# Layer 0's first FFN output projection: both halves token-major, the last half turned behind a joint gate pair

## The chip, the cores and the metric

The kernel runs on one core of a Trainium2 chip. The metric is the device time of one execution in microseconds (us); the time before is the median of 3 runs. TensorE (PE) multiplies, its weight load (PEld) overlaps the product before; VectorE (DVE), ScalarE (ACT) and GpSimd (POOL) do the elementwise work; SyncE (SP) issues nearly all DMAs. Weights come from DRAM, products are summed in PSUM banks of 512 fp32 columns.

## The reference

A two-layer decoder trunk on 256 tokens of width 1024. Cut to what matters here, layer 0 is

```python
h = h + 0.5 * swiglu_ffn(rmsnorm(h, ffn1_norm[0]), ffn1_w_in[0], ffn1_w_out[0])   # (silu(gate) * up) @ w_out
hn = rmsnorm(h, mix_norm[0])
b_gate, c_gate, v = jnp.split(hn @ conv_w_in, 3, axis=-1)
u = c_gate * v
y = causal_conv3(u, conv_w)            # width 3, one filter per channel
h = h + (b_gate * y) @ conv_w_out
h = h + 0.5 * swiglu_ffn(rmsnorm(h, ffn2_norm[0]), ffn2_w_in[0], ffn2_w_out[0])
```

Layer 1 has a shared K/V projection, two FFNs of the same kind and sparse attention in place of the convolution. d_ff is 2816, which is 22 blocks of 128.

## The kernel before

**Number format.** Every fp32 product is made of three: each operand is split into a high part rounded to fp32r and the rest, and high x high, rest x high and high x rest are summed. A weight "unit" is 128 x 1024 fp32 weights as such a pair (wh, wl).

**Weights.** The class `Stream` (object `W`) loads chunks of two units (1 MB) from DRAM into three buffers `ws` by SP (L139), rounds a unit on ScalarE (`high`, CAST, L166) and takes the rest on VectorE (`low`, L183). Six units are held at most. `W.take()` hands one to the products, `W.done(n, pump)` gives buffers free and, unless told not to, calls `W.pump()`, which rounds units until the buffers are full; a chunk's load is issued when the last unit of the chunk two before it is rounded. All engines run their instructions in the order in which the program writes them (a manual schedule), so a place in the code is a place in each engine's queue.

**Two forms of product.** Channel-major: a weight tile of 128 x 128 stands in the array and all 256 tokens of both parts of the activations pass (512 columns, L539), then the weight's rest with the high parts (256 columns, L545). Token-major: 128 tokens stand in the array and 512 weight columns pass, three times (L485 to L487 in `out_proj`). A token-major result has tokens on partitions and must be turned: VectorE transposes blocks of 32 x 32 (L493), two DMAs write the tile to DRAM (`back`, L494), two read it back with channels on partitions (`come`, L513), and `joined(m)` adds channel tiles 2m and 2m+1 to the residual `h` (L520).

**Layer 0's first output projection.** `out_proj` with `rest` and without `whole`: `half` makes the first 512 channels token-major; tiles 4 to 7 of the other 512 are channel-major, each evacuated from PSUM by `out_evac` (L455), with `come` and `joined(0)`, `joined(1)` put between them. Layer 1's first projection (which comes after layer 0's second FFN) already runs with `whole=True`: both halves token-major, `joined(2)` and `joined(3)` called later, between joint products of the K/V projection, where each channel gets two sets of norm inputs (`xkv` and `xs`).

**The norm.** `Norm.high` and `Norm.low` write the scaled activations `xs[c]` in two parts (L294 on ScalarE, L298 on VectorE); `squares` squares on ScalarE (L309) and sums on GpSimd (L311); `halves` splits the sum (L317, L318 on GpSimd); `rows` sums over channels on TensorE (L327) and takes the root and the reciprocal R (L329, L331).

**The convolution's products.** Four token-major groups (c_gate and v, `conv_tokens`, 8 channel tiles k each, one unit per two k), each in a pair of PSUM banks `mm` of which there are two pairs, then eight channel-major tiles for b_gate. `conv_step(n, k)` puts the side work into these loops: the norm's rows in group 0 and the DMA round trip that makes the column form r2 of R (L774, L775), `conv_turned` (evacuates, scales with r2, transposes, L747 to L752), `placed` (reads back), `conv_taps` (the filter).

Of the kernel before, what the change touches and what calls it, by code (L numbers as in the profile page):

```python
# [16 lines left out]
P = 128  # L17
T = 256
# [50 lines left out]
def trunk(ctx, tc, A, out):  # L69
# [30 lines left out]
    def bank2():  # L100
        return mk([P, 2, 512], "mm", 2, pool=ps)
# [366 lines left out]
        if c == ND - 1:  # L468
            norm.low(c)

    def out_proj(lhs, factor, norm, rest=None, cut=(7, 7, 7, 2), whole=False):

        n, i, u = len(lhs), 0, None

# [35 lines left out]
        def come(new=t2):  # L510
            for m in range(2):
                came.append(new([P, 2, T], F32))
                sy.dma_start(came[m].rearrange("p c (b j) -> p c b j", j=32),  # L513
                             d[m].rearrange("t (b i) (x c j) -> (i x) c (t b) j", i=32, c=2, j=32))

        def joined(m):
            cs = range(2 * m, 2 * m + 2)
            u = came.pop(0)
            for c in cs:
                ve.scalar_tensor_tensor(out=h[c], in0=u[:, c % 2], scalar=factor, in1=h[c], op0=ALU.mult, op1=ALU.add)  # L520
            for c in cs:
                norm.high(c)
            for c in cs:
                norm.squares(c)
                norm.low(c)
# [22 lines left out]

        if whole:
            d = half(lambda k: come() if k == 6 else joined(k // 3 - 4) if k in (12, 15) else None)  # L550
            W.pump()
            come(act)
            return joined

        c = 4
# [163 lines left out]
    hid, rest = ffn_tokens(xs, rc=rc, n0=2, hid=hid, old=old)  # L719
    xs = new_xs()  # L720
    nm = Norm([(xs, G_MIX)])
    out_proj(hid, 0.5, nm, rest=rest)
    nm.halves()

    zs, Y, conv = [], [], {}
    tab = tables()
# [1 line left out]
    def conv_tokens(o, step):  # L728

        for k in range(8):  # L730
            if k % 2 == 0:
                u, = W.take()
            wh, wl = [u[x][:, (k % 2) * 512:(k % 2 + 1) * 512] for x in range(2)]
            for tt in range(2):
                sh, sl = xs[k][:, tt * P:(tt + 1) * P], xs[k][:, T + tt * P:T + (tt + 1) * P]
                pe.matmul(o[:, tt], sh, wh, start=(k == 0), stop=False)  # L736
                pe.matmul(o[:, tt], sl, wh, start=False, stop=False)
                pe.matmul(o[:, tt], sh, wl, start=False, stop=(k == 7))  # L738
            if k % 2 == 1:
                W.done(1, k < 7)  # L740
            step(k)

    def conv_turned(o):
        tb = t2([P, 2, T])
        for tt in range(2):
            g = t1()
            ac.copy(g, o[:, tt, :T])  # L747
            ve.scalar_tensor_tensor(out=g, in0=o[:, tt, T:], scalar=conv["r2"][:, tt:tt + 1], in1=g,
                                    op0=ALU.mult, op1=ALU.mult)
# [18 lines left out]
        po.tensor_tensor(out=y, in0=y, in1=conv["R"], op=ALU.mult)  # L768

    def conv_step(n, k):  # L770
        if (n, k) == (0, 5):
            conv["R"] = R = nm.rows()
            rd, rc, conv["r2"] = mk([1, T], "rd", 1, pool=dr), mk([P, 2], "rc", 2, pool=tiny), sm([P, 2])
            sy.dma_start(rd, R[:1])  # L774
            sy.dma_start(rc, rd.rearrange("o (t p) -> (o p) t", t=2))  # L775
            po.tensor_tensor(out=conv["r2"], in0=rc, in1=rc, op=ALU.mult)
        if (n, k) in ((1, 1), (2, 2)):
            next(tab)
        if (n, k) == (1, 4):
            way.append(conv_turned(conv.pop("o")))  # L780
        if (n, k) in ((2, 0), (2, 4), (3, 3)):
            conv["u"].append(placed(way.pop(0)))
        if (n, k) in ((2, 6), (3, 0), (3, 4), (3, 6)):
            conv_taps(taps.pop(0))

    conv["u"], way, taps = [], [], list(range(4))
    for n in range(4):
        o = bank2()
        conv_tokens(o, lambda k: conv_step(n, k))
        if n == 0:  # L790
            conv["o"] = o
        else:
            way.append(conv_turned(o))
        W.pump()
    bs = {}

# [4 lines left out]
    for f in range(8):  # L801
        o, (u,) = bank(), W.take()
        a_pass([(o, u, xs, range(8))])
        W.done(1, False)
        if f == 1:
            conv["u"].append(placed(way.pop()))
        if f:
            conv_split(f - 1)
        if f in (0, 1):
            conv_taps(4 + f)  # L810
        bs[f] = b = t1()
        ac.copy(b, o[:, T:])
        ve.tensor_tensor(out=b, in0=o[:, :T], in1=b, op=ALU.add)
        ve.tensor_tensor(out=b, in0=b, in1=Y[f // 2][:, f % 2], op=ALU.mult)  # L814
        if f == 7:
            conv_split(7)
        W.pump()
        if f in (4, 5):
            conv_taps(2 + f)
    conv.clear()  # L820
    del o, u, b

# [7 lines left out]
    def load_bias(j):  # L830
        pp, hg = divmod(j, 4)
        b = kt8[:, j, T:].rearrange("p (a n) -> p a n", a=2)
        src = bass.AP(tensor=row_d.tensor, offset=row_d.offset + (8 * pp + hg) * OHW,
                      ap=[[1, P], [4 * OHW, 2], [1, 256]])
        for a in range(2):
            if a == 0:
                sy.dma_start(b, src)
        bias[j] = b

    def c_bias(j):  # L840
# [15 lines left out]
    xk_a = mk([P, 4, 512], "kt", 1, F32R)  # L856
    xkv = [xk_a[:, k] for k in range(4)] + [t2(dt=F32R) for _ in range(4)]
    nm = Norm([(xkv, G_KV), (xs, G_FFN1 + 8)])
    joined = out_proj(hid, 0.5, nm, rest=rest, whole=True)
    del hid  # L860

    def b_full(xk, mid=None, shadow=None, o=None):
# [626 lines left out]
def _layout(i):  # L1489
# [3 lines left out]
    for n in ("ffn1", "ffn2"):  # L1493
        w = a[n + "_w_in"]
        ins, outs = [], []
        for w, v, turn in zip(w.reshape(2, 1024, -1), a[n + "_w_out"], ((0, 0), (2, 1))[n == "ffn2"]):
            ins.append(w.reshape(8, 128, 2, NF // 2, 256).transpose(1, 3, 0, 2, 4).reshape(128, -1))
            v = v.reshape(-1, 4, 2, 32, 1024).transpose(0, 2, 3, 1, 4).reshape(-1, 1024)
            if turn == 2:
                v = v.reshape(NF, 128, 2, 2, 2, 32, 4).transpose(1, 2, 0, 3, 6, 4, 5)  # L1500
                outs.append(v.reshape(128, -1))
                continue
            if turn:
                outs.append(v.reshape(NF, 128, 2, 512).transpose(1, 2, 0, 3).reshape(128, -1))
                continue
            first = v[:, :512].reshape(FF, 2, 2, 32, 4).transpose(0, 1, 4, 2, 3).reshape(NF, 128, 512).transpose(1, 0, 2)
            v = v[:, 512:].reshape(NF, 128, 4, 128).transpose(1, 2, 0, 3)
            outs.append(np.concatenate([x.reshape(128, -1) for x in (first, v)], 1))
        r[n + "_w_in"], r[n + "_w_out"] = np.stack(ins), np.stack(outs)
# [2 lines left out]
    rows, second = np.concatenate([x, w[:, 0]], 2).reshape(128, -1), w[:, 1].reshape(128, -1)  # L1512
    w = a["conv_w_in"][0]
    cv = w[:, 1024:].reshape(8, 128, 2, 4, 2, 32, 4).transpose(1, 3, 0, 2, 6, 4, 5).reshape(128, -1)
    r["conv_w_in"] = np.concatenate([cv, _rows(w[:, :1024])], 1)
    r["conv_w_out"] = _rows(a["conv_w_out"][0])
    w = a["w_kv"].reshape(8, 128, 3, 2, 256)
    full = w[:, :, 1:].transpose(1, 0, 3, 2, 4).reshape(128, 2, -1)
# [50 lines left out]
```

## Time and profile before

| what | value |
|---|---|
| median of 3 runs | 948.61 us (948.56 to 948.75) |
| the profiled execution | 949.32 us, its span 947.5 us |
| granted TensorE clock | 1.00 |
| busy: PE, PEld, DVE, ACT, POOL | 943.3, 787.0, 653.2, 531.9, 113.1 us |
| moved by DMA | 209.48 MB, mean 221 GB/s |

How to read it: times in rows are microseconds from the span's start. A row of the timeline has its start, its duration, the engine, the line, the operation, out<-in and how many instructions are merged; in brackets the idle time before it and who ended it. A matmul's duration is its latency, and matmuls overlap; the pace is read from stretches. A row of a DMA issue has the count, the size of each and the median time from issue to landing.

### The profile page before, as it was taken

The page shows a single profiled execution, that of the slowest core. Times are in us where ns is not written, and L with a number is a line of the kernel's source. Part 1 is how long each engine was busy: PE and PEld are TensorE (multiplying, and loading weights), DVE is VectorE, ACT ScalarE, POOL GpSimd, SP SyncE. Part 2 cuts the span into 40 slices and gives each one's busy share as a digit, 9 for nine tenths or more (in the row PEclk, how much of TensorE's full clock was granted, in tenths as well). Part 3 has the DMA queues.
Part 4 walks back from the last instruction along what each step waited for, and adds up shares of the span by engine and source line. Part 5 has one row for each costly group of instructions (what it writes and reads, how often), then busy time and mean ns, then how long its engine had stood idle before and what let it go on. Part 6 is the DMA issues. An engine that isn't in the chain of part 4 may idle for free.

```text
span 947.5 us, 12702 instructions
## 1 busy us (share of the span) xinstructions
PE 943.3 (100%) x4566; PEld 787.0 (83%) x4566; DVE 653.2 (69%) x1064; ACT 531.9 (56%) x895; POOL 113.1 (12%) x191
## 2 busy tenths in 40 slices
PE   9999999999999999999999999999999999999998
PEld 8888888888888888888888888888877888888887
DVE  7776755777896667745776676866679787766652
ACT  7555544555565545544667775644589765445440
POOL 2000000211020000000231022200237120000000
PEclk9999999999999999999999999999999999999999
DMA  8788787558636998777656887867511248998760
GB/s 313 238 250 278 232 265 224 210 184 261 221 146 235 258 274 265 234 277 227 217 221 201 262 243 246 268 247 217 193 44 41 94 178 254 277 298 251 248 226 23
DMA packets 168572, 209.48 MB, mean 221 GB/s; under 512 B 128396, under 2 KB 145421, under 8 KB 148030
## 3 DMA queue, kind: packets, MB, share of 16 engines
q1 hardware_dynamic: 168366, 208.42, 67.9%
q8 instruction: 36, 0.59, 0.2%
q10 hardware_dynamic: 144, 0.26, 0.1%
q14 instruction: 26, 0.21, 0.1%
HBM read 191.32 MB, written 16.81 MB: 220 GB/s over the span
## 4 chain that ended last, share of the span: by engine, by line
PE 99%; ACT 0%; DVE 0%; issue 0%
PE mm L434 16%; PE mm L432 16%; PE mm L433 16%; PE a L539 5%; PE mm L486 4%; PE mm L487 4%; PE mm L485 4%; PE a L351 3%; PE a L545 3%; PE mm L668 2%; PE a L604 2%; PE a L603 2%; PE a L602 2%; PE a L356 2%; PE mm L736 2%; PE mm L738 2%
## 5 line engine op out<-in xcount | busy, mean ns | idle before, releaser
L183 DVE TENSOR_TENSOR wl<-ws,wh 128x1024 fp32r<-128x1024 f32 x316 | 387.7, 1247 | 214.7 <-ACT wh L166 200.8
L166 ACT CAST wh<-ws 128x1024 fp32r<-128x1024 f32 x316 | 325.4, 1048 | 240.8 <-DMA ws<-in_ffn_w_in_dram 101.3
L432 PE MATMUL mm<-wh,xs 128*128 128x512 f32 x656 | 255.9, 390 | 0.0
L434 PE MATMUL mm<-wl,xs 128*128 128x512 f32 x656 | 255.4, 389 | 0.0
L433 PE MATMUL mm<-wh,xs 128*128 128x512 f32 x656 | 255.3, 389 | 0.0
L434 PEld LDWEIGHTS mm<-wl,xs 128*128 128x128 f32 x656 | 123.1, 188 | 25.9 <-DVE wl L183 0.4
L433 PEld LDWEIGHTS mm<-wh,xs 128*128 128x128 f32 x656 | 123.2, 188 | 25.4
L432 PEld LDWEIGHTS mm<-wh,xs 128*128 128x128 f32 x656 | 123.2, 188 | 25.2
L311 POOL TENSOR_TENSOR sq<-sq,t 128x256 f32<-128x256 f32 x42 | 34.8, 828 | 398.2 <-ACT t L309 397.4
L390 ACT ACTIVATE t<-mm,rc 128x256 f32<-128x256 f32 x86 | 40.7, 473 | 55.6 <-DVE t L391 48.5
L485 PE MATMUL mm<-wh,act 128*128 128x512 f32 x176 | 68.5, 389 | 0.0
L486 PE MATMUL mm<-wh,act 128*128 128x512 f32 x176 | 68.5, 389 | 0.0
L487 PE MATMUL mm<-wl,act 128*128 128x512 f32 x176 | 68.5, 389 | 0.0
L391 DVE SCALAR_TENSOR_TENSOR t<-mm,rc,t 128x256 f32<-128x256 f32 x86 | 41.4, 482 | 14.9 <-ACT t L390 11.3
L294 ACT ACTIVATE xs<-base 128x256 fp32r<-128x256 f32 x48 | 24.0, 505 | 45.9 <-DVE base L455 33.5
L539 PE MATMUL a<-act,wh 128*128 128x512 f32 x208 | 49.0, 390 | 0.0
L539 PEld LDWEIGHTS a<-act,wh 128*128 128x128 f32 x208 | 38.5, 188 | 7.7
L359 ACT CAST act<-t 128x256 fp32r<-128x256 f32 x96 | 34.5, 405 | 15.4 <-DVE t L814 9.1
L392 DVE STREAM_TRANSPOSE t<-t 128x256 f32<-128x256 f32 x88 | 39.2, 446 | 3.1
L485 PEld LDWEIGHTS mm<-wh,act 128*128 128x128 f32 x176 | 33.0, 188 | 6.9
L486 PEld LDWEIGHTS mm<-wh,act 128*128 128x128 f32 x176 | 33.0, 188 | 6.8
L487 PEld LDWEIGHTS mm<-wl,act 128*128 128x128 f32 x176 | 33.0, 188 | 6.8
(301 smaller groups left out, 1213.1 us busy)
## 6 DMA issues: line engine op xcount, KB each, us to landing
ws<-in_ffn_w_in_dram SPq DMA_DIRECT2D x84, 1024.0 KB, 6.2
ws<-in_ffn_w_out_dram SPq DMA_DIRECT2D x44, 1024.0 KB, 5.9
turn<-t SPq DMA_DIRECT2D x48, 256.0 KB, 2.3
t<-turn SPq DMA_DIRECT2D x48, 256.0 KB, 7.0
ws<-in_conv_w_in_dram SPq DMA_DIRECT2D x12, 1024.0 KB, 5.1
ws<-in_w_kv_dram SPq DMA_DIRECT2D x6, 1024.0 KB, 6.1
ws<-in_conv_w_out_dram SPq DMA_DIRECT2D x4, 1024.0 KB, 5.1
ws<-in_attn_w_q_dram SPq DMA_DIRECT2D x4, 1024.0 KB, 5.1
```

The costliest lines, as they stand in the source:

```text
L166: ac.copy(h, src)
L183: ve.tensor_tensor(out=l, in0=src, in1=h.bitcast(F32), op=ALU.subtract)
L390: ac.activation(s, o[tt][:, :T], AF.Silu, scale=rc[:, tt:tt + 1])
L391: ve.scalar_tensor_tensor(out=s, in0=o[tt][:, T:], scalar=rc[:, tt:tt + 1], in1=s, op0=ALU.mult, op1=ALU.mult)
L392: ve.transpose(tb[:, tt], s)
L432: pe.matmul(o[tt], sh, wh, start=(k == 0), stop=False)
L433: pe.matmul(o[tt], sl, wh, start=False, stop=False)
L434: pe.matmul(o[tt], sh, wl, start=False, stop=(k == 7))
L485: pe.matmul(o[:, tt], sh, wh, start=(k == 0), stop=False)
L486: pe.matmul(o[:, tt], sl, wh, start=False, stop=False)
L487: pe.matmul(o[:, tt], sh, wl, start=False, stop=(k == NF - 1))
L539: pe.matmul(o, run[k][0], lhs[k], start=(k == 0), stop=(k == last))
```

## The change

Layer 0's first projection is called with `whole=1`. Both halves are token-major; the second half's reads (`come(act)`) are issued ahead of the weight rounding that follows (for `whole=2`, which layer 1's call now passes, behind it as before). The weights' layout in DRAM follows. The first two of the four convolution groups become one joint loop over eight k, one whole unit per k, 12 products for it: `pair`, in one `mm` pair of banks and two single banks. `joined(2)` and `joined(3)` stand behind k = 1 and 2; `nm.halves()` and the rounding of three units behind k = 3; no other unit is rounded until k = 5, where the norm's rows, the r2 round trip and then the rounding of the next units follow. The side work moves: both turned groups of the pair at (2, 1) and (2, 2), the reads, tables and taps later. The bias tiles 0 to 3 of the second FFN are loaded by two DMAs each instead of one.

```diff
-    def out_proj(lhs, factor, norm, rest=None, cut=(7, 7, 7, 2), whole=False):
+    def out_proj(lhs, factor, norm, rest=None, cut=(7, 7, 7, 2), whole=0):
...
         if whole:
             d = half(lambda k: come() if k == 6 else joined(k // 3 - 4) if k in (12, 15) else None)
+            if whole == 2:
+                W.pump()
+            come(act)
             W.pump()
-            come(act)
             return joined
...
-    out_proj(hid, 0.5, nm, rest=rest)
-    nm.halves()
+    joined = out_proj(hid, 0.5, nm, rest=rest, whole=1)
+    del hid
...
     def conv_step(n, k):
-        if (n, k) == (0, 5):
+        if (n, k) == (1, 5):
             conv["R"] = R = nm.rows()
...
-        if (n, k) in ((1, 1), (2, 2)):
+        if (n, k) in ((2, 0), (3, 0)):
             next(tab)
-        if (n, k) == (1, 4):
-            way.append(conv_turned(conv.pop("o")))
-        if (n, k) in ((2, 0), (2, 4), (3, 3)):
+        if (n, k) in ((2, 1), (2, 2)):
+            way.append(conv_turned(pair.pop(0)))
+        if (n, k) in ((2, 4), (2, 6), (3, 3)):
             conv["u"].append(placed(way.pop(0)))
-        if (n, k) in ((2, 6), (3, 0), (3, 4), (3, 6)):
+        if (n, k) in ((3, 1), (3, 2), (3, 4), (3, 6)):
             conv_taps(taps.pop(0))

     conv["u"], way, taps = [], [], list(range(4))
-    for n in range(4):
+    pair = [bank2(), [bank(), bank()]]
+    pair[0] = [pair[0][:, tt] for tt in range(2)]
+    for k in range(8):
+        u, = W.take()
+        for x, o in enumerate(pair):
+            wh, wl = [w[:, x * 512:(x + 1) * 512] for w in u]
+            for tt in range(2):
+                sh, sl = xs[k][:, tt * P:(tt + 1) * P], xs[k][:, T + tt * P:T + (tt + 1) * P]
+                pe.matmul(o[tt], sh, wh, start=(k == 0), stop=False)
+                pe.matmul(o[tt], sl, wh, start=False, stop=False)
+                pe.matmul(o[tt], sh, wl, start=False, stop=(k == 7))
+        W.done(1, k > 5)
+        if k in (1, 2):
+            joined(k + 1)
+        elif k == 3:
+            nm.halves()
+            W.pump(3)
+        conv_step(1, k)
+        if k == 5:
+            W.pump()
+    for n in (2, 3):
         o = bank2()
+        o = [o[:, tt] for tt in range(2)]
         conv_tokens(o, lambda k: conv_step(n, k))
-        if n == 0:
-            conv["o"] = o
-        else:
-            way.append(conv_turned(o))
+        way.append(conv_turned(o))
         W.pump()
...
-        if f in (0, 1):
-            conv_taps(4 + f)
+        if f in (0, 1, 6):
+            conv_taps(4 + f // 2 + f % 2)
...
-        if f in (4, 5):
-            conv_taps(2 + f)
+        if f == 4:
+            conv_taps(6)
...
         for a in range(2):
-            if a == 0:
-                sy.dma_start(b, src)
+            if a == 0 or j < 4:
+                sy.dma_start(b[:, a:] if j > 3 else b[:, a], src[:, a:] if j > 3 else src[:, a])
...
-    joined = out_proj(hid, 0.5, nm, rest=rest, whole=True)
+    joined = out_proj(hid, 0.5, nm, rest=rest, whole=2)
```

Three places in the engines' queues. First SP, around the end of the projection and the start of the convolution's groups, before: `back` and `t` are the first half's write and read, `ws` a weight load, `rd` and `rc` the round trip of R.

```order
L494 DMA back_1380<-pr_1381 128x2x256
L494 DMA back_1380<-pr_1384 128x2x256
L139 DMA ws_1424<-in_ffn_w_out_dram 128x2048
L513 DMA t_284_1446<-back_1380 128x16x32
L513 DMA t_285_1448<-back_1380 128x16x32
L139 DMA ws_1496<-in_conv_w_in_dram 128x2048
L139 DMA ws_1522<-in_conv_w_in_dram 128x2048
L139 DMA ws_1605<-in_conv_w_in_dram 128x2048
L139 DMA ws_1644<-in_conv_w_in_dram 128x2048
L139 DMA ws_1677<-in_conv_w_in_dram 128x2048
L139 DMA ws_1715<-in_conv_w_in_dram 128x2048
L774 DMA rd_1742<-R_1740 1x256
```

And now, from the last load ahead of the second half's write (`back_1600`) and read (`act`) to the loads behind the round trip:

```order
L139 DMA ws_1568<-in_conv_w_in_dram 128x2048
L494 DMA back_1600<-pr_1601 128x2x256
L494 DMA back_1600<-pr_1604 128x2x256
L513 DMA act_1607<-back_1600 128x16x32
L513 DMA act_1609<-back_1600 128x16x32
L139 DMA ws_1613<-in_conv_w_in_dram 128x2048
L139 DMA ws_1701<-in_conv_w_in_dram 128x2048
L776 DMA rd_1740<-R_1738 1x256
L777 DMA rc_1741<-rd_1740 128x2x1
L139 DMA ws_1748<-in_conv_w_in_dram 128x2048
L139 DMA ws_1758<-in_conv_w_in_dram 128x2048
```

A second pair of writes and reads has come in, with no weight load between the writes and the reads; two loads now follow the round trip directly.

VectorE from the last evacuation of the projection to the reciprocal, before (`wl` is a unit's rest, `base` the residual):

```order
L455 SCALAR_TENSOR_TENSOR base<-a_1609,base 128x256 x2
L298 SCALAR_TENSOR_TENSOR xs_1189<-base,xs_1189 128x256
L183 TENSOR_TENSOR wl_1679<-ws_1605,wh_1675 128x1024
L183 TENSOR_TENSOR wl_1699<-ws_1644,wh_1697 128x1024
L183 TENSOR_TENSOR wl_1717<-ws_1644,wh_1713 128x1024
L183 TENSOR_TENSOR wl_1733<-ws_1677,wh_1731 128x1024
L331 RECIPROCAL R_1740<-t_329_1738 128x256
```

And now, from the last transpose of the second half:

```order
L493 STREAM_TRANSPOSE pr_1604<-mm_1391 128x512
L183 TENSOR_TENSOR wl_1615<-ws_1522,wh_1611 128x1024
L520 SCALAR_TENSOR_TENSOR base<-act_1607,base 128x256 x2
L298 SCALAR_TENSOR_TENSOR xs_1186<-base,xs_1186 128x256
L298 SCALAR_TENSOR_TENSOR xs_1187<-base,xs_1187 128x256
L520 SCALAR_TENSOR_TENSOR base<-act_1609,base 128x256 x2
L298 SCALAR_TENSOR_TENSOR xs_1188<-base,xs_1188 128x256
L298 SCALAR_TENSOR_TENSOR xs_1189<-base,xs_1189 128x256
L183 TENSOR_TENSOR wl_1697<-ws_1568,wh_1695 128x1024
L183 TENSOR_TENSOR wl_1703<-ws_1568,wh_1699 128x1024
L183 TENSOR_TENSOR wl_1707<-ws_1613,wh_1705 128x1024
L331 RECIPROCAL R_1738<-t_333_1736 128x256
```

The additions of channels 4 to 7 wait for DMAs (`act`) instead of PSUM, and all four stand between the transposes and the rounding of the next three units.

ScalarE from the root of the norm (`a_1735`) to the copies of the first turned group (`mm_1684`), before:

```order
L329 ACTIVATE t_329_1738<-a_1735,epst 128x256
L166 CAST wh_1760<-ws_1677 128x1024
L166 CAST wh_1779<-ws_1715 128x1024
L166 CAST wh_1803<-ws_1715 128x1024
L747 COPY t_346_1816<-mm_1684 128x256
L747 COPY t_347_1820<-mm_1684 128x256
```

And now, to the copies of the pair's first group (`mm_1617`):

```order
L329 ACTIVATE t_333_1736<-a_1733,epst 128x256
L166 CAST wh_1746<-ws_1613 128x1024
L166 CAST wh_1752<-ws_1701 128x1024
L166 CAST wh_1756<-ws_1701 128x1024
L166 CAST wh_1774<-ws_1748 128x1024
L166 CAST wh_1790<-ws_1748 128x1024
L166 CAST wh_1817<-ws_1758 128x1024
L749 COPY t_357_1822<-mm_1617 128x256
L749 COPY t_358_1826<-mm_1617 128x256
```

Three more casts stand ahead of the copies, and they read the loads `ws_1748` and `ws_1758` that SP issues behind the round trip.

More of the change, by code (lines that the diff above doesn't have):

```diff
@@ L735, in conv_tokens @@
                 sh, sl = xs[k][:, tt * P:(tt + 1) * P], xs[k][:, T + tt * P:T + (tt + 1) * P]
-                pe.matmul(o[:, tt], sh, wh, start=(k == 0), stop=False)
-                pe.matmul(o[:, tt], sl, wh, start=False, stop=False)
-                pe.matmul(o[:, tt], sh, wl, start=False, stop=(k == 7))
+                pe.matmul(o[tt], sh, wh, start=(k == 0), stop=False)
+                pe.matmul(o[tt], sl, wh, start=False, stop=False)
+                pe.matmul(o[tt], sh, wl, start=False, stop=(k == 7))
             if k % 2 == 1:
@@ L746, in conv_turned @@
             g = t1()
-            ac.copy(g, o[:, tt, :T])
-            ve.scalar_tensor_tensor(out=g, in0=o[:, tt, T:], scalar=conv["r2"][:, tt:tt + 1], in1=g,
+            ac.copy(g, o[tt][:, :T])
+            ve.scalar_tensor_tensor(out=g, in0=o[tt][:, T:], scalar=conv["r2"][:, tt:tt + 1], in1=g,
                                     op0=ALU.mult, op1=ALU.mult)
@@ L776, in conv_step @@
             po.tensor_tensor(out=conv["r2"], in0=rc, in1=rc, op=ALU.mult)
-        if (n, k) in ((1, 1), (2, 2)):
+        if (n, k) in ((2, 0), (3, 0)):
             next(tab)
-        if (n, k) == (1, 4):
-            way.append(conv_turned(conv.pop("o")))
-        if (n, k) in ((2, 0), (2, 4), (3, 3)):
+        if (n, k) in ((2, 1), (2, 2)):
+            way.append(conv_turned(pair.pop(0)))
+        if (n, k) in ((2, 4), (2, 6), (3, 3)):
             conv["u"].append(placed(way.pop(0)))
-        if (n, k) in ((2, 6), (3, 0), (3, 4), (3, 6)):
+        if (n, k) in ((3, 1), (3, 2), (3, 4), (3, 6)):
             conv_taps(taps.pop(0))
     conv["u"], way, taps = [], [], list(range(4))
-    for n in range(4):
+    pair = [bank2(), [bank(), bank()]]
[6 more added lines that the diff above has]
+                sh, sl = xs[k][:, tt * P:(tt + 1) * P], xs[k][:, T + tt * P:T + (tt + 1) * P]
+                pe.matmul(o[tt], sh, wh, start=(k == 0), stop=False)
+                pe.matmul(o[tt], sl, wh, start=False, stop=False)
+                pe.matmul(o[tt], sh, wl, start=False, stop=(k == 7))
+        W.done(1, k > 5)
[8 more added lines that the diff above has]
+    for n in (2, 3):
         o = bank2()
+        o = [o[:, tt] for tt in range(2)]
         conv_tokens(o, lambda k: conv_step(n, k))
-        if n == 0:
-            conv["o"] = o
-        else:
-            way.append(conv_turned(o))
+        way.append(conv_turned(o))
         W.pump()
@@ L1495, in _layout @@
         ins, outs = [], []
-        for w, v, turn in zip(w.reshape(2, 1024, -1), a[n + "_w_out"], ((0, 0), (2, 1))[n == "ffn2"]):
+        for w, v, turn in zip(w.reshape(2, 1024, -1), a[n + "_w_out"], ((2, 0), (2, 1))[n == "ffn2"]):
             ins.append(w.reshape(8, 128, 2, NF // 2, 256).transpose(1, 3, 0, 2, 4).reshape(128, -1))
@@ L1514, in _layout @@
     cv = w[:, 1024:].reshape(8, 128, 2, 4, 2, 32, 4).transpose(1, 3, 0, 2, 6, 4, 5).reshape(128, -1)
-    r["conv_w_in"] = np.concatenate([cv, _rows(w[:, :1024])], 1)
+    pair = cv[:, :8192].reshape(128, 2, 8, 512).transpose(0, 2, 1, 3).reshape(128, -1)
+    r["conv_w_in"] = np.concatenate([pair, cv[:, 8192:], _rows(w[:, :1024])], 1)
     r["conv_w_out"] = _rows(a["conv_w_out"][0])
```

## The prediction

> **What bounds the kernel now.** I read the page first (span, busy time, chain), then who TensorE waited for, then the stretches on both sides of the place that is changed.
>
> ```profile
> span 947.5 us, 12702 instructions
> PE 943.3 (100%) x4566; PEld 787.0 (83%) x4566; DVE 653.2 (69%) x1064; ACT 531.9 (56%) x895; POOL 113.1 (12%) x191
> PE 99%; ACT 0%; DVE 0%; issue 0%
> ...
> PE a L250 <- PEq L1558: 0.8, 1, 0.8
> PE a L1315 <- ACT xs L1325: 0.4, 1, 0.4
> ```
>
> The reader is to see that the chain that ends last is TensorE alone, and that in the whole program it waits twice, for 1.2 us together, neither time near the first output projection. So there is no stall here to remove: the time can fall only by fewer or cheaper matmuls, and rise only by a new wait of TensorE. The profiled execution took 949.32 us, 0.71 above the median of the runs, 948.61; I sum against it and carry the difference over to the median.
>
> **Part 1: the second half becomes token-major.** The stretches of the two halves (each: length, PE busy and count, and so on), and the matmul groups in the second:
>
> ```profile
> 125.68:155.60 29.92, 29.92 (x134) 24.78 (x132) 17.12 (x20) 13.46 (x18) 0.00 (x0) 1.00 0.72 238
> 155.60:186.14 30.54, 30.54 (x178) 27.06 (x176) 20.66 (x30) 16.33 (x25) 4.69 (x6) 1.00 0.59 186
> ...
> L539 PE MATMUL a<-act,wh 128*128 128x512 f32 x88 | 20.5, 390 | 0.0
> L545 PE MATMUL a<-act,wl 128*128 128x256 f32 x88 | 11.0, 283 | 0.0
> ```
>
> The token-major half is 132 matmuls of 512 columns (two more in the count are neighbours cut by the edges) in 29.92 us, 226.7 ns each. The channel-major half is 88 of 512 and 88 of 256 in 30.54: taking 88 x 226.7 ns = 19.95 off leaves 10.59 / 88 = 120.3 ns for one of 256. Half the columns cost 7 ns more than half the time, so each matmul carries some 13 to 14 ns that do not shrink with it, and 44 fewer matmuls for the same columns save 30.54 - 29.92 = **0.62 us**. The new half has the form, operands and count of the old first half, so this is a measured difference. It lies wholly on the path.
>
> The Trainium skill (TensorE: Matmul & The Clock Gate, Back-to-back issue gap) gives N/2.4 + 2.5 ns between starts on the warm clock, with a constant far smaller than the rows' 13 to 14 ns. By it 44 fewer matmuls would save 44 x 2.5 ns = 0.11 us instead of 0.62. The granted clock in the rows is 1.00 and the difference of two whole stretches decides, so I stay with 0.62.
>
> On the other engines four evacuations are removed (out_evac's two additions from PSUM each); two transposes, two writes, two reads and four additions of a returned tile come in, and the norm's work per channel stays. VectorE has 20.66 busy in 30.54 us there and is not the bound; six rounded weight units, 12 matmuls = 2.72 us each, cover its short delays. The first half's own way back now ends in the second half: its additions stand ahead of products 12 and 15, 16.3 and 20.4 us in, for reads that by the rows of part 2 land near 10; nothing.
>
> **Part 2: the way back of the last half.** Before, the last channels were ready on chip. Now channels 4 to 7 go PSUM, transpose, DRAM, back, addition, norm, behind the first units of the gate pair. Zero is the pair's first matmul. Unit k starts at 2.72 k: channel 4 is needed at 10.88 (its low part one 0.23 later), channel 6 at 16.32, and the norm's rows matmul, in order behind unit 5, also at 16.32.
>
> How far the way is until the reads start, from the old first half (ended 155.60): transposes, writes, reads.
>
> ```profile
> 155.80 1.31 DVE L493 STREAM_TRANSPOSE pr<-mm 128x512 f32<-128x512 f32 x2 [0.63 <-PE mm L487]
> ...
> 156.54 0.98 SPq L494 DMA_DIRECT2D back<-pr  x2
> 157.61 0.45 SPq L139 DMA_DIRECT2D ws<-in_ffn_w_out_dram  x1
> 159.69 3.43 SPq L513 DMA_DIRECT2D t<-back  x2
> ```
>
> The first read is issued at 159.69 - 155.60 = 4.09. What a 256 KB read in 128-byte pieces takes to land (last column), for single reads and for the old pair:
>
> ```profile
> t<-turn SPq DMA_DIRECT2D x1, 256.0 KB, 3.4
> t<-turn SPq DMA_DIRECT2D x1, 256.0 KB, 4.4
> t<-back SPq DMA_DIRECT2D x2, 256.0 KB, 6.3
> ```
>
> The old pair of reads had a 1 MB weight load (157.61) queued ahead on SP. Now the next weight load is emitted behind the reads and the one before them early, so I take the middle of the single reads, 3.9: landed at **8.0**, bounds 7.5 and 10.4. Channel 4 needs the addition, the scaled copy and the rest after it, 1.5 us by the layer-1 rows below (465.24 to 466.24 + 0.48): 9.5, before 10.88.
>
> Layer 1 has the same way back already, with two norm sets per channel:
>
> ```profile
> 465.24 0.76 DVE L520 SCALAR_TENSOR_TENSOR base<-act,base 128x256 f32<-128x256 f32 x2 [2.39 <-DMA act<-back]
> 466.24 0.48 DVE L298 SCALAR_TENSOR_TENSOR t<-base,t 128x256 fp32r<-128x256 f32 x1 [0.24 <-ACT t L294]
> 466.64 0.48 DVE L298 SCALAR_TENSOR_TENSOR xs<-base,xs 128x256 fp32r<-128x256 f32 x1
> 467.84 1.85 DVE L520 SCALAR_TENSOR_TENSOR base<-act,base 128x256 f32<-128x256 f32 x2
> ...
> 469.73 0.51 ACT L294 ACTIVATE t<-base 128x256 fp32r<-128x256 f32 x1
> 470.15 0.50 ACT L294 ACTIVATE xs<-base 128x256 fp32r<-128x256 f32 x1
> 470.55 0.71 ACT L309 ACTIVATE t<-base 128x256 f32<-128x256 f32 x2
> ...
> 467.79 1.62 POOL L311 TENSOR_TENSOR sq<-sq,t 128x256 f32<-128x256 f32 x2 [13.72 <-ACT t L309]
> 471.09 1.61 POOL L311 TENSOR_TENSOR sq<-sq,t 128x256 f32<-128x256 f32 x2 [1.68 <-ACT t L309]
> 472.76 1.28 POOL L317 CAST act<-sq 128x256 fp32r<-128x256 f32 x1
> 474.12 1.60 POOL L318 TENSOR_TENSOR act<-sq,act 128x256 fp32r<-128x256 f32 x1
> ```
>
> From the first addition (465.24) to the split sum of squares (474.12 + 1.60) is 10.48 us. Layer 0 has one set: two of the four rest operations at a step of 0.40 fall away (0.80) and one scaled copy ahead of the last squares (470.15 to 470.55, 0.40): 10.48 - 1.20 = 9.3. So GpSimd ends at 8.0 + 9.3 = 17.3, and the rows matmul, due at 16.32, waits **0.95 us**. Queued behind it on TensorE is unit 6, so all of it is lost. Bounds: with the first landing at 7.5 and GpSimd's cast at its lower value, 0.88 less (0.40 for 1.28, next row), the end is 15.9 and the wait 0; landing at 10.4 makes 19.7 and a wait of 3.4 (channel 4 late by 0.8 at 11.9 - 11.11 is part of it).
>
> ```profile
> L317 POOL CAST act<-sq x2: 397/836/1276, 189.8 to 472.8; 128x256 fp32r<-128x256 f32 x2
> ```
>
> I take the upper value, since three weight units are rounded on VectorE just behind the halves, as in layer 1 where the cast took 1.28. The pair 465.24 / 467.84 shows the same: two additions in 0.76 us alone, in 1.85 beside GpSimd. The Trainium skill (GPSIMD Engine Reference, Specifications) says that GpSimd shares its SBUF interfaces with VectorE and contends with instructions that have two SBUF inputs. The rounding has two, so by this rule too the late value holds, and the rival without a wait gets less.
>
> The rounding itself: unit 6 must be ready at 16.5. The three casts follow the last square, in layer 1 at 471.2, 3.4 behind 467.84; here the last square ends near 12.8, the first unit is rounded 1.05 + 1.55 later, 15.4. Covered. On SP the loads of units 8 to 11 are queued behind the waiting reads; the second read is issued near 4.7, the loads some 3 us later (3.43 for the issue of both reads above), and land near 13.5, while unit 8 is due at 22.0: nothing.
>
> **Part 3: what hangs on the rows.** The reciprocal goes to DRAM and back and scales the turned gate groups, which free the bank of the third group of the rest:
>
> ```profile
> 194.33 0.40 PE L327 MATMUL a<-act,ones 128*128 128x256 f32 x2
> ...
> 196.71 0.48 ACT L329 ACTIVATE t<-a,epst 128x256 f32<-128x256 f32 x1
> ...
> 197.21 1.75 DVE L331 RECIPROCAL R<-t 128x256 f32<-128x256 f32 x1 [0.56 <-ACT t L329]
> 204.95 0.48 DVE L748 SCALAR_TENSOR_TENSOR t<-mm,sm,t 128x256 f32<-128x256 f32 x1
> 205.87 0.48 DVE L748 SCALAR_TENSOR_TENSOR t<-mm,sm,t 128x256 f32<-128x256 f32 x1
> ...
> 200.61 0.41 SPq L139 DMA_DIRECT2D ws<-in_conv_w_in_dram  x1
> ...
> ws<-in_conv_w_in_dram SPq DMA_DIRECT2D x1, 1024.0 KB, 5.2
> ws<-in_conv_w_in_dram SPq DMA_DIRECT2D x1, 1024.0 KB, 7.0
> ```
>
> On SP two weight loads stand behind the round trip, and on ScalarE three casts of those loads now stand ahead of the copies of the turned group. From the rows' start r: 0.40 + 0.48 + 1.75, with up to 0.5 for VectorE's last rounding, makes the reciprocal r + 2.7 to 3.2; the first load is issued 1.65 later (198.96 to 200.61), the second 0.45 behind, landing 7.0 on: r + 11.8 to 12.3. Then cast 1.05, rest 1.23 and 205.87 + 0.48 - 204.95 = 1.40: r + 15.5 to 16.0. The last group's first matmul needs the bank at r + 0.23 + 24 x 0.2267 + 48 x 0.2267 = r + 16.55. Slack 0.5 to 1.0, cost 0; bound above 0.8 if the second load lands 1.3 late.
>
> The tables, the taps of the convolution and the turned groups' reads move back by about one group. Their first consumer is the evacuation of the first of the last eight tiles, whose bank TensorE wants again four tiles later, 4 x 8 x (226.7 + 120.3) ns = 11.1 us: cost 0, bound 1.0 above.
>
> Four more DMAs of the bias tiles (four issues split in two) stand on SP in the next FFN: at 0.3 to 0.6 us per issue in the rows above and with units rounded ahead, nothing; bound 0 to 0.3. The joint order of the pair's matmuls has the same count and form: nothing.
>
> **Sum:** 948.61 - 0.62 + 0.95 = **948.9** us.
>
> **Rivals.**
> - No wait at all: first landing near 7.5 and the short cast. 948.61 - 0.62 = 948.0. For it: a single read of 3.4. Against: VectorE is rounding beside it.
> - Slower: the read back takes the old 6.3, as when a load stands ahead. Channel 4 and the rows wait 3.4 together, 951.4. It decides from a total wait of 2.5 us, a first landing later than 9.5. Against: no load is queued ahead.
> - The copies of the turned group come late behind the casts that wait for weights: up to 0.8 more, 949.7. For it: a slack of 0.5 to 1.0 that rests on one load.
> - Faster by more than 0.2%: needs 1.9 us where the rows show 0.62 to gain.
> - The change does not do on TensorE what it says: the new half takes as long as the old, the saving is 0 and the wait stays: 949.6. Against: the first half's row. The Trainium skill's formula of part 1 would lie near this one.
>
> **How the numbers follow.** 0.2%, 1.9 us, is about what a measurement of this kernel can tell from no change. Chances: the forecast (wait 0.4 to 1.8, 948.4 to 949.8) 0.46, no wait 0.30, slow read 0.10, late copies 0.10, no saving 0.02, faster 0.02. The range from 947.9 (no wait, with 0.1 of scatter) to 950.4 holds the first, second and most of the fourth, and the lower waits of the third. Within 0.2%: 0.87. Slower: 0.11, the slow read and the tail of the late copies. Faster: 0.02.
>
> **What would show it.** 132 matmuls in 29.9 us in the second half; a PE wait of about 1 us before L327 with GpSimd as releaser; no wait at channel 4; the copy and scaling of the first turned group ending before the last group starts. A wait at channel 4, or more than 2 us at the rows, would make the prediction wrong, as would a new wait in a later stage.

## The result and the profile after

The changed kernel takes **954.12 us**, median of 6 runs (953.10 to 954.86), beside 948.87 of the kernel before in the same comparison: ratio 1.0054, 95% interval 1.0041 to 1.0067. It is 5.25 us slower, and outside the range of the prediction. The profiled execution took 953.13 us, near the lowest of its runs. Its page, and who TensorE waited for:

```profile
span 951.3 us, 12620 instructions
PE 943.5 (99%) x4522; PEld 784.2 (82%) x4522; DVE 654.1 (69%) x1062; ACT 531.5 (56%) x895; POOL 115.6 (12%) x191
PE 92%; DVE 4%; DMA 3%; issue 1%; ACT 1%; DVEq 0%; ACTq 0%; SPq 0%
...
PE a L351 <- DVE act L360: 2.5, 2, 1.8
PE a L351 <- DVE t L833: 1.1, 2, 0.6
```

The chain that ended last was all TensorE before; now 8% of it is VectorE, DMA and issue. TensorE waits 3.6 us in L351, for operands that VectorE splits (L360) and for PSUM banks that VectorE evacuates (L833): these are the eight tiles of b_gate and the convolution's output projection, two stages that begin 44 us and more behind the end of the changed half. The stretches by stage, after (both halves, pair and two groups, eight tiles, output projection) and before (the last three):

```profile
125.08:155.00 29.92, 29.92 (x134) 24.77 (x132) 17.51 (x20) 14.09 (x19) 0.00 (x0) 1.00 0.73 256
155.00:184.92 29.92, 29.92 (x134) 24.77 (x132) 17.97 (x21) 14.29 (x19) 2.22 (x3) 1.00 0.67 211
184.92:228.92 44.00, 44.00 (x195) 36.26 (x194) 31.39 (x42) 22.88 (x35) 8.48 (x12) 1.00 0.67 213
228.92:252.14 23.22, 22.71 (x129) 19.77 (x128) 20.80 (x35) 12.66 (x25) 4.74 (x6) 1.00 0.79 250
252.14:278.40 26.26, 23.18 (x131) 19.49 (x130) 22.52 (x42) 14.94 (x26) 4.69 (x6) 1.00 0.46 164
```

```profile
186.14:229.95 43.81, 43.81 (x197) 36.29 (x196) 32.54 (x41) 22.88 (x31) 7.39 (x11) 1.00 0.73 246
229.95:252.26 22.31, 22.31 (x129) 19.66 (x128) 21.44 (x40) 14.52 (x27) 3.44 (x5) 1.00 0.71 223
252.26:274.56 22.30, 22.30 (x130) 19.65 (x129) 17.22 (x32) 11.94 (x21) 3.54 (x5) 1.00 0.40 147
```

The halves save 30.54 - 29.92 = 0.62 us as summed. The groups lose 0.19, the tiles 0.91, the output projection **3.96**. Together +4.44; the profiled spans differ by 3.8, since the work ahead of the change ended 0.60 earlier in this execution (125.08 against 125.68). The medians differ by 5.25; the rest of that is in executions slower than the profiled one, and the last section has what is known of them.

Where the tiles come late. ScalarE in the changed kernel, around the end of the last turned group:

```profile
227.76 0.51 ACT L766 ACTIVATE act<-t,base 128x256 f32<-128x256 f32 x1
232.55 1.05 ACT L166 CAST wh<-ws 128x1024 fp32r<-128x1024 f32 x1 [4.28 <-DMA ws<-in_conv_w_in_dram]
233.51 0.50 ACT L766 ACTIVATE act<-t,base 128x256 f32<-128x256 f32 x1
...
237.83 0.36 ACT L832 COPY t<-a 128x256 f32<-128x256 f32 x1
```

A weight cast stands 4.28 us for its load; behind it in the same queue are a tap (L766), the group's copies and the first tile's copy (237.83). VectorE after, and before (the first and the eighth tile's addition, the last split; after with the reciprocal, whose row of before stands in the prediction):

```profile
202.41 1.74 DVE L331 RECIPROCAL R<-t 128x256 f32<-128x256 f32 x1
...
239.61 0.42 DVE L833 TENSOR_TENSOR t<-a,t 128x256 f32<-128x256 f32 x1
...
259.61 0.41 DVE L833 TENSOR_TENSOR t<-a,t 128x256 f32<-128x256 f32 x1
261.03 0.43 DVE L360 TENSOR_TENSOR act<-t,act 128x256 fp32r<-128x256 f32 x1 [0.47 <-ACT act L359]
```

```profile
234.51 0.42 DVE L813 TENSOR_TENSOR t<-a,t 128x256 f32<-128x256 f32 x1
...
254.27 0.41 DVE L813 TENSOR_TENSOR t<-a,t 128x256 f32<-128x256 f32 x1
255.68 0.43 DVE L360 TENSOR_TENSOR act<-t,act 128x256 fp32r<-128x256 f32 x1 [0.47 <-ACT act L359]
```

The reciprocal ends 5.2 us later (204.15 against 198.96), the first tile is added 5.1 later, the last split is 5.35 later. In this execution the lateness is as large at the end of the 57 us as at their start.

### The profile page after: what moved, and what is told of

It reads as the page before. It is cut to its first block, busy times and chain, and to the rows that moved or that the text cites. A ratio compares the mean times of both kernels' runs of the same rounds, so it can differ in the third digit from the quotient of the medians.

```text
span 951.3 us, 12620 instructions
## 1 busy us (share of the span) xinstructions
PE 943.5 (99%) x4522; PEld 784.2 (82%) x4522; DVE 654.1 (69%) x1062; ACT 531.5 (56%) x895; POOL 115.6 (12%) x191
## 4 chain that ended last, share of the span: by engine, by line
PE 92%; DVE 4%; DMA 3%; issue 1%; ACT 1%; DVEq 0%; ACTq 0%; SPq 0%
PE mm L432 16%; PE mm L434 16%; PE mm L433 16%; PE mm L487 5%; PE mm L486 5%; PE mm L485 5%; PE a L539 3%; PE mm L670 2%; PE a L606 2%; PE a L604 2%; PE a L605 2%; PE a L351 2%; PE a L545 2%; DVE wl L183 1%; DMA ws<-in_conv_w_in_dram 1%; PE mm L1290 1%
## 5 line engine op out<-in xcount | busy, mean ns | idle before, releaser
L485 PE MATMUL mm<-wh,act 128*128 128x512 f32 x220 | 85.6, 389 | 0.0
L486 PE MATMUL mm<-wh,act 128*128 128x512 f32 x220 | 85.6, 389 | 0.0
L487 PE MATMUL mm<-wl,act 128*128 128x512 f32 x220 | 85.6, 389 | 0.0
L486 PEld LDWEIGHTS mm<-wh,act 128*128 128x128 f32 x220 | 41.3, 188 | 8.6
L485 PEld LDWEIGHTS mm<-wh,act 128*128 128x128 f32 x220 | 41.3, 188 | 8.6
L487 PEld LDWEIGHTS mm<-wl,act 128*128 128x128 f32 x220 | 41.3, 188 | 8.5
L360 DVE TENSOR_TENSOR act<-t,act 128x256 fp32r<-128x256 f32 x96 | 37.0, 423 | 1.0 <-ACT act L359 1.0
L605 PE MATMUL a<-wh,act 128*128 128x512 f32 (+1 forms) x90 | 34.6, 384 | 0.0
```

The costliest lines, as they stand in the source:

```text
L487: pe.matmul(o[:, tt], sh, wl, start=False, stop=(k == NF - 1))
L605: pe.matmul(o, sl, wh, start=False, stop=False)
```

## The experiments

Three readings were open: **A**, the cast that waits ahead of the tile; **B**, the taps and turned groups themselves, late; **R**, the reciprocal's round trip ahead of the weight loads on SP.

**1. The cast behind the tile.** In the last turned group no unit is rounded from k = 5 on; it is done behind the first tile.

```diff
-        conv_tokens(o, lambda k: conv_step(n, k))
+        conv_tokens(o, lambda k: conv_step(n, k), 7 if n == 2 else 5)   # W.done(1, k < stop)
...
-        W.pump()
+        if n == 2:
+            W.pump()
...
-        W.pump()
+        W.pump(2 if f < 2 else NBUF)
```

> The fifth and sixth weight unit of the last eight tiles (their load lands at 232.45 us) are not rounded during the last turned group but behind the evacuation of the first tile. Theory A (ScalarE runs in order, and its cast stands waiting for this load ahead of tap 3, the last turned group's copies and the first tile's copy): the idle 4.28 us ahead of the cast go, the copies of the last turned group come 2 to 3 us earlier; then tap 4, whose read lands at 234.85, gates the first tile's copy, now near 235.3 instead of 237.8: some 2 to 2.5 us regained, about 951.7. Theory B (the taps and turned groups themselves come late, the cast only stands beside them): tap 4 and the tables set the same times, regained 0 to 0.5, about 953.8. Theory R (the round trip of the reciprocal ahead of the weight loads on SP is the root): the load is as late as before, 0 to 2 regained.

954.51 us, ratio 1.0062 (1.0049 to 1.0074): nothing regained. The cast's wait went and the next took its place, ScalarE's row:

```profile
237.62 0.51 ACT L766 ACTIVATE act<-t,base 128x256 f32<-128x256 f32 x1 [2.59 <-DMA t<-turn]
238.04 0.35 ACT L833 COPY t<-a 128x256 f32<-128x256 f32 x1
```

Tap 4 now waits for its read, which by this row landed near 237.6 and not at 234.85, as had been expected; the first tile's copy is at 238.04 instead of 237.83, in an execution whose tiles start 0.68 later (229.60 against 228.92).

**2. The taps later.** Taps 4 and 5 at the third and fourth tile (`f in (2, 3, 6)`, `conv_taps(7 if f == 6 else 2 + f)`).

> Taps 4 and 5 are made two tiles later (ahead of the evacuations of the third and fourth of the eight tiles instead of the first and second). Theory A: the cast that waits until 232.45 and the last turned group's copies behind it stay ahead of the first evacuation; only tap 4's copy (some 0.4 to 1.5 us) goes from in front of it, and comes back two tiles later: 0 to 1.5 regained, about 953. Theory B: the first tile's copy no longer waits for the read of tap 4 at 234.85, most of 5.25 us regained, about 949.5. Theory R: 0 to 1.5.

954.63 us, ratio 1.0065 (1.0051 to 1.0078). Now the cast waits alone: its row reads 3.63 us for the load. B by itself falls.

**3. Both.**

> The edits of the two runs ahead together. Theory A and B alike, if the late evacuation of the first tile is what costs the conv's output projection its 4 us: the first tile is evacuated near 233 to 234 us as in the kernel before, nearly all is regained, 948.87 - 0.62 + 0.2 = 948.4, up to 949.5 if the taps moved later now make the products late. If the loss comes from elsewhere (the fourth product's operands, the loads of the output projection), 953 to 954.

952.72 us, ratio 1.0041 (1.0029 to 1.0054): a miss for A and B alike. The first tile is added at 235.61, 1.1 behind the kernel before, and the eight tiles take 22.32 us with no wait, yet the output projection is still 4.17 longer than 22.30. The first tile was not what sets the end.

**4. The round trip on ScalarE's queue** (`ac.dma_start` for rd and rc).

> The two DMAs of the reciprocal's round trip are issued on ScalarE's queue instead of SP's, so that the weight loads behind them on SP start some 3 to 5 us earlier. Theory R: the casts at 210.60 and 213.15 no longer wait, the first turned group is copied 3 to 4 us earlier, all that follows on SP moves up as much, and most of the 5.25 us are regained, 949 to 950. Theory A and B alone (the order within the last turned group decides): the late load behind the turned groups' reads stays late, 0 to 1.5 regained, 953 to 954; ScalarE itself may stand 2 us in the second issue, which waits for the first DMA.

953.61 us, ratio 1.0047 (1.0035 to 1.0060): next to nothing regained. The three loads behind the round trip, in the changed kernel and here, and here the cast that waits for the second of them:

```profile
205.75 2.10 SPq L139 DMA_DIRECT2D ws<-in_conv_w_in_dram  x3
```

```profile
200.75 9.87 SPq L139 DMA_DIRECT2D ws<-in_conv_w_in_dram  x3
```

```profile
212.82 1.05 ACT L166 CAST wh<-ws 128x1024 fp32r<-128x1024 f32 x1 [2.29 <-DMA ws<-in_conv_w_in_dram]
```

Only the first load was issued earlier, by 5.0 us; the other two came later than before (208.02 and 210.29 instead of 206.30 and 207.52), because ScalarE stood 3.41 us on the round trip ahead of the casts and VectorE's rests that free their buffers. The first group's copy came at 213.78 instead of 214.11. So this run does not give R the early loads that it asked for, and does not decide on it.

What the four have in common is VectorE. Summed over the rows of its timeline between the reciprocal's end and the last split, it is, before, 47.93 us busy and 9.22 idle, after 48.02 and 9.29, with 20 roundings in both. **Theory C**: that stage is VectorE's; the reciprocal starts it, and its end gives TensorE its last banks and operands. The row of a window (length, VectorE busy) shows it in the kernel before:

```profile
226.00:256.00 30.00, 27.72 (x50) 1.00 0.74 243
```

VectorE is 92% busy there, while TensorE never waits.

**5. Units 6 and 7 rounded in the pair's first two units**, in VectorE's idle 5.06 us (`W.done(1, k < 2 or k > 5)`).

> New theory C, formed from the four runs ahead: behind the reciprocal VectorE has a fixed amount of work up to the last operand of the conv's output projection (20 roundings, four turned groups, eight taps, eight evacuations), 48.0 us busy and about 9.3 us idle in the kernel before and in the changed one alike; it ends 57.2 us behind the reciprocal in both, the reciprocal ends 5.2 us later now, and TensorE has to wait for the last operands. Here units 6 and 7 are rounded in the pair's first two units, in VectorE's idle 5.06 us ahead of the returned tiles, not behind the norm. Theory C: one rounding fewer stands behind the reciprocal (1.2 us) and the next load is emitted ahead of the reciprocal's round trip, so that up to 4.2 us of idle time go: last operand near 256.5 to 258 instead of 261.46, the time 949.0 to 950.5. Theory B (late taps and turned groups by themselves): they hang on the reciprocal, which stays: 953 to 954.

951.56 us, ratio 1.0027 (1.0016 to 1.0039). 2.6 us regained, more than B allowed and less than C's 3.6 to 5.1, so a miss for both. There is one rounding fewer behind the reciprocal, but 8.88 us stay idle there, 2.61 of it for a cast that waits 4.62 for its load. The edit also brings three loads instead of two ahead of the round trip on SP, so a share of what it regains may be R's; no run takes that apart.

**6. The kernel before with 12 idle products behind the reciprocal.**

```diff
             conv["R"] = R = nm.rows()
+            g = t1()
+            for _ in range(12):
+                ve.tensor_tensor(out=g, in0=R, in1=R, op=ALU.mult)
```

> The kernel before, with 12 extra multiplications of 128x256 on VectorE right behind the reciprocal (some 0.42 us each, 5.0 us in all; the product is used by nobody, and nothing else is moved). Theory C: the kernel before had no slack on VectorE worth naming though TensorE never waits there: the last operand comes some 4 to 5 us later, near 260 to 261, TensorE waits in the conv's output projection, 952.5 to 954.5. Theory A or B (a cast that stands for a load, or late taps, and not the amount of work): VectorE's 9.2 us of idle time behind the reciprocal take the 5 us up, 948.9 to 949.5.

950.54 us, ratio 1.0018 (1.0009 to 1.0027): slower, but C had said 3.6 to 5.6 us and it is 1.6.

```profile
198.86 5.50 DVE L775 TENSOR_TENSOR t<-R 128x256 f32<-128x256 f32 x12
```

```profile
209.64 0.47 PE L736 MATMUL mm<-wh,xs 128*128 128x512 f32 x1 [1.50 <-DVE t L748]
```

The 5.50 us are there; idle time behind the reciprocal fell from 9.22 to 5.69, so 3.5 were absorbed, and 1.5 reached TensorE at the bank of a turned group. The output projection stayed at 22.30. VectorE's idle time early in the stage can be used; C as "no slack anywhere" was too strong.

**7. The changed kernel without one of the two additions of each tap** (`for a in range(1, 2)`; the oldest neighbour is left out of the convolution).

> The changed kernel with one of the two additions of each tap of the convolution left out (the oldest neighbour is not added): 8 operations of some 0.45 us fewer on VectorE behind the reciprocal, 3.6 to 4.0 us, and no data any earlier. Theory C: the last operand comes 3 to 4 us earlier, near 257.5 to 258.5, and TensorE's waits of 3.6 us go nearly all: 949.3 to 950.5. Theory A or B: the casts, loads, reads and taps wait as before, 953 to 954.

951.41 us, ratio 1.0025 (1.0016 to 1.0034), 2.7 regained with no data any earlier. The last split ends at 258.75, the projection takes 24.16. A and B had said that nothing would change; C had said 949.3 to 950.5, which the median misses by 0.9; the last section bears on this.

**8. The pair alone**: the old second half, its weights laid out as before, the norm's rows at the pair's third unit.

```diff
-    joined = out_proj(hid, 0.5, nm, rest=rest, whole=1)
+    out_proj(hid, 0.5, nm, rest=rest)
+    nm.halves()
...
-        if (n, k) == (1, 5):
+        if (n, k) == (1, 2):
...
-        W.done(1, k > 5)
-        if k in (1, 2):
-            joined(k + 1)
-        elif k == 3:
-            nm.halves()
-            W.pump(3)
+        W.done(1)
...
-        if k == 5:
-            W.pump()
```

> The changed kernel with the old second half (channel-major, weights laid out as before, no way back), the norm's rows at the pair's third unit, and units rounded as they come free: the joint pair and the new order of turned groups and taps alone. Theory C: the reciprocal ends near 199 as in the kernel before; the turned groups can only start behind the pair, near 208, so VectorE has some 2 us more idle time ahead of them; last operand 256 to 258, the time 948.9 to 951. If the pair's order itself (late turned groups, clustered taps) costs the time, whatever the reciprocal does: 953 to 954.

950.73 us, ratio 1.0019 (1.0010 to 1.0029). The reciprocal ends at 199.25 as before, VectorE idles 10.55 us behind it instead of 9.22, the last split ends at 258.24. So by the medians the pair's order costs 1.8 us. The profiled execution (950.22) shows 0.35 of this in the output projection; where the rest lies is open. The other 3.4 go with what this edit takes away: the turned half (its saving of 0.62 included), the late reciprocal and the rounding that is held back in the pair.

**9. Experiments 1, 2 and 5 together.**

> The edits of the first, second and fifth experiment together, the likeliest way to win the time back with the result unchanged. The nine traces so far follow one line: the conv's output projection is longer than its 22.30 us by what its last operand is later than 5.25 us behind its first matmul. Theory C: one rounding fewer behind the reciprocal (1.2 us), VectorE's idle 2.6 us ahead of the waiting cast gone: last operand 257.0 to 259.5, some 5.5 to 8 us behind the projection's start, so 0.3 to 2.8 us of waits are left; 949.0 to 951.5. If the edits only move the same idle time (as the second experiment did): as the fifth experiment, 951.6.

949.68 us beside 949.17 before, ratio 1.0004 (0.9995 to 1.0012): 4.7 of the 5.25 us are back. Idle time behind the reciprocal is 6.27. One wait of TensorE is left in these stages:

```profile
256.89 1.43 PE L351 MATMUL a<-act,wh 128*128 128x512 f32 x5 [0.63 <-DVE t L834]
```

**10. As 9, the tiles' product on GpSimd** (`po.tensor_tensor(out=b, in0=b, in1=Y...)`).

> The run ahead with the eight tiles' product with the convolution on GpSimd instead of VectorE (0.42 to 0.75 us each on VectorE; a product of this shape takes 0.74 on GpSimd). Theory C: 3.4 us of work leave VectorE; beside GpSimd its two-input operations took up to 0.33 us more, 2.6 us given back at worst: last operand 0.8 to 3.4 us earlier than in the run ahead, 948.3 to 950.5, the lower end below the kernel before. Against it: the chain of each tile gets 0.3 to 0.6 us longer and the last operand itself waits for it, 0 to 0.6 later than the run ahead.

953.64 us, ratio 1.0049 (1.0036 to 1.0062): a miss, 4 us worse than 9. GpSimd and VectorE rows where both work:

```profile
246.45 1.72 POOL L835 TENSOR_TENSOR t<-t,act 128x256 f32<-128x256 f32 x1
```

```profile
245.86 1.71 DVE L183 TENSOR_TENSOR wl<-ws,wh 128x1024 fp32r<-128x1024 f32 x1
248.64 0.43 DVE L360 TENSOR_TENSOR act<-t,act 128x256 fp32r<-128x256 f32 x1 [1.07 <-ACT act L359]
```

Beside a rounding the product takes 1.72 us instead of 0.74, the rounding 1.71 instead of 1.21, and VectorE, in order, stands 1.07 ahead of a split that waits for the product by way of ScalarE's cast. The Trainium skill (GPSIMD Engine Reference, Specifications) says that GpSimd shares its SBUF interfaces with VectorE and contends with its instructions of two SBUF inputs; these rows agree.

**11. The kernel before with one idle product behind each of the eight tiles.**

> The kernel before with one extra product of 128x256 on VectorE behind each of the eight tiles' evacuations (used by nobody), 8 of 0.42 us, a step of 0.34 to 0.42 each: 2.7 to 3.4 us where VectorE has next to no idle time. Theory C: last operand 2.7 to 3.4 us later, 6.55 to 7.25 behind the start of the projection instead of 3.85, so 1.3 to 2.0 us of waits where there were none; 950.2 to 951.0. If VectorE is not what sets the end there: 948.9 to 949.2, no wait.

950.88 us, ratio 1.0018 (1.0009 to 1.0027), as C had it: last split 7.04 behind the projection's start, the projection 1.67 longer.

**12. As 9, the last tap behind the eighth tile's addition** (`if f == 7: conv_taps(7)` between addition and product).

> The ninth experiment's kernel, with the last tap made behind the eighth tile's first addition instead of ahead of the seventh tile's evacuation. In the ninth, TensorE still waits 0.6 us for the eighth tile's bank (added at 256.43, wanted at 255.84) and some 0.5 us ahead of it. Theory C: that addition comes some 1.2 us earlier, near 255.2, the waits go; the eighth operand comes up to 0.7 us later, near 259.0, 7.2 behind the projection's start, where TensorE wants it only 8.2 behind it, so nothing waits: the part that the changed half saves is left, before - 0.62 + 0.2 = 948.4 to 948.9, 0.4 less than before. If the last operand's lateness over 5.25 us counts by itself (the line of the nine traces taken as a law), 2 us of waits and 950.5.

948.98 us beside 949.02 before, ratio 1.0002 (0.9993 to 1.0011). The waits of TensorE in the whole program, and the eighth tile's addition:

```profile
PE a L250 <- PEq L1582: 0.8, 1, 0.8
PE a L1338 <- ACT xs L1348: 0.4, 1, 0.4
PE a L327 <- POOL act L318: 0.3, 1, 0.3
```

```profile
255.10 0.42 DVE L834 TENSOR_TENSOR t<-a,t 128x256 f32<-128x256 f32 x1
```

The waits in L351 are gone; the last split, at 258.67 still 7.13 behind the start, costs nothing, so it was the bank and not the last operand that TensorE stood for. The loss is undone; the 0.62 saved are given back: pair and groups take 44.31 us (+0.50), the output projection 22.62 (+0.32). No version beats the kernel before by more than can be told apart.

All traces in one table. TensorE wants the eighth tile's bank 18 x 0.2267 = 4.08 us after the projection's start; "bank late" is the end of that tile's addition less the start less 4.08; "longer" is the projection over 22.30.

| kernel | reciprocal ends | bank late, us | projection longer, us |
|---|---|---|---|
| before | 198.96 | -1.66 | 0.00 |
| after | 204.15 | 3.80 | 3.96 |
| 1 | 204.83 | 3.98 | 4.83 * |
| 2 | 204.58 | 4.46 | 4.63 |
| 3 | 204.70 | 3.32 | 4.17 * |
| 4 | 204.06 | 3.82 | 3.99 |
| 5 | 204.27 | 3.38 | 4.04 * |
| 6 | 198.75 | -1.43 | 0.00 |
| 7 | 204.45 | 1.71 | 1.86 |
| 8 | 199.25 | 0.19 | 0.35 |
| 9 | 204.68 | 1.00 | 1.14 |
| 10 | 204.20 | 5.15 | 5.30 |
| 11 | 199.02 | 1.53 | 1.67 |
| 12 | 204.46 | -0.10 | 0.32 |

Without the starred rows (below, on the clock) the two columns agree within 0.17 us wherever the bank is late, and in each of those traces the first product into that bank starts 0.05 to 0.06 us after the addition's end. The waits for the fifth and sixth operands (0.62 and 1.84 in the changed kernel) lie ahead of it and are no second cost: the bank is later still.

## Why the prediction was wrong, step by step

- **Part 1** held: 29.92 for 30.54, 0.62 saved. The Trainium skill's gap constant (TensorE: Matmul & The Clock Gate, Back-to-back issue gap), by which it would have been 0.11, does not fit these rows. The page gives it for a single matmul in isolation, and says of a stream that matmul and weight load together set the spacing.
- **Part 2** was right in kind, too large in price. No wait at channel 4. The reads were issued 3.77 after the pair's start (forecast 4.09), the first addition ran at +7.67 (8.0), GpSimd ended at +16.48 (17.3):

```profile
192.59 0.76 DVE L520 SCALAR_TENSOR_TENSOR base<-act,base 128x256 f32<-128x256 f32 x2 [5.06 <-DMA act<-back]
...
216.29 0.48 DVE L750 SCALAR_TENSOR_TENSOR t<-mm,sm,t 128x256 f32<-128x256 f32 x1
```

```profile
188.69 2.60 SPq L513 DMA_DIRECT2D act<-back  x2
```

```profile
198.46 1.27 POOL L317 CAST act<-sq 128x256 fp32r<-128x256 f32 x1
199.81 1.59 POOL L318 TENSOR_TENSOR act<-sq,act 128x256 fp32r<-128x256 f32 x1
```

```profile
201.24 0.61 PE L327 MATMUL a<-act,ones 128*128 128x256 f32 x2
```

The first of the two rows products ran when it was due, 184.92 + 16.32 = 201.24; the second waited some 0.2 us for GpSimd instead of 0.95; the long cast (1.27) was foreseen.

- **Part 3, the copies of the turned group**: forecast r + 15.5 to 16.0 against a need at r + 16.55. With r = 201.24 the scaling (216.29 + 0.48 above) that frees the bank ended at 216.77, r + 15.5; TensorE did not wait. Right.
- **The step that failed** is part 3's next sentence: "The tables, the taps of the convolution and the turned groups' reads move back by about one group. Their first consumer is the evacuation of the first of the last eight tiles, whose bank TensorE wants again four tiles later ... cost 0, bound 1.0". The first bank is wanted at 228.92 + 11.1 = 240.0 and was free at 239.61 + 0.42 = 240.03; the next cost 0.5, and the tiles' 0.91 lie within the bound. But the price was taken at the first consumer alone. The same lateness goes on through eight evacuations and splits that VectorE does one behind another, and arrives at the eighth bank and the output projection's operands, where the kernel before had 4.08 - 2.42 = 1.66 us to spare. That bank came 7.88 us behind the projection's start instead of 2.42, 5.46 later; less the 1.66 it is 3.80 late, of 3.96 lost. The sum of a moved step must run to the last consumer on that engine, and the slack there was to be read from rows of before: VectorE 27.72 of 30.00 us busy. That the lateness was not bound to arrive whole is shown by 12, whose reciprocal is as late.
- **Rivals**: the late turned copies had casts that wait for weights, at another place, and a price of up to 0.8. "A new wait in a later stage" was named as what would make it wrong, without a price or a chance. The dearest rival, a slow read, was priced at 951.4; none reached 954.

Shown by runs: the loss follows the eighth bank (table), less VectorE work regains half of it (7), more work makes such a loss in the kernel before (11), and rearranging that work undoes it (9, 12). By 8, about a third of the median's loss is the pair's order, though its trace shows only 0.35 us of that, and the rest comes with the turned half, its late reciprocal and the held-back rounding; these three were not taken apart, but 5 puts 2.6 us on rounding two units earlier, with the load that this brings ahead of the round trip. How much of the loss the round trip ahead of the loads (R) makes is open. Not tried: an earlier reciprocal with the turned half kept, since the returned tiles stand ahead of it.

## What to carry to other kernels

When a change makes one small result later (here a norm's reciprocal), count what the engine behind it still has to do up to its last consumer, and compare with the time left there; a stage in which TensorE never waits can still have an engine 92% busy with 1.7 us to spare. An engine's idle time counts only where its work can be moved into it: two single fixes (1 and 2) did nothing because each uncovered the other's wait, while both together with the filled idle stretch ahead of the reciprocal won 4.7 us. Moving work to GpSimd to relieve VectorE made both slower.

## What the hardware showed that was not expected

A wait of TensorE can be followed by a second cost. In experiment 3 it waits 1.84 us, and the clock granted to it (third value from the end) falls to 0.70 and 0.50 in the windows behind:

```profile
255.37 6.00 PE L351 MATMUL a<-act,wh 128*128 128x512 f32 x18 [1.84 <-DVE act L360]
```

```profile
254.00:256.00 2.00, 0.63 (x3) 0.54 (x4) 1.97 (x4) 1.90 (x4) 0.00 (x0) 1.00 0.10 25
256.00:258.00 2.00, 2.00 (x8) 1.60 (x7) 1.90 (x4) 0.57 (x2) 0.74 (x1) 0.70 0.96 319
258.00:260.00 2.00, 2.00 (x6) 1.54 (x6) 1.63 (x4) 0.34 (x2) 0.00 (x0) 0.50 0.43 180
260.00:262.00 2.00, 2.00 (x13) 1.77 (x12) 1.27 (x2) 1.12 (x2) 0.00 (x0) 0.95 0.00 0
```

18 products take 6.00 us where 13 and 5 took 3.25 and 1.43 in the changed kernel's execution, whose clock stayed at 1.00 through waits of 0.62, 1.84 and 0.63. The starred rows of the table have this dip, and their projection is 0.66 to 0.85 us longer than the bank explains (10 has it too, under the wait for a bank that came later anyway). Whether an execution has it differs: the mean granted clock of the changed kernel is 1.000 in the two executions of 953.1 us and 0.996 to 0.998 in three of the other four; in experiment 7 seven executions at 1.000 took 949.79 to 951.97 (median 950.43, which C had allowed) and four at 0.998 took 952.53 to 953.13. The kernel before, and experiments 6 and 11 made from it, never fell below 0.999.

The Trainium skill (TensorE: Matmul & The Clock Gate, Part 1: The HAM clock gate) has the clock halved behind an idle window of about 3.4 us. The halving agrees. The length does not: here a wait of 1.84 us, with a shorter pause and one product ahead of it, was followed by it in some executions. Why in some and not in others is not shown.
